# Last 256 tokens of a transformer layer: LayerNorm weights ahead of the transposes, sums on TensorE, mean taken off while the power is made

## The chip, the cores and the metric

The kernel runs on one core of one Trainium2 chip. A core has five engines with queues of their own: TensorE (PE in the profile; its weight loads are PEld), VectorE (DVE), ScalarE (ACT), GpSimd (POOL) and SyncE (SP, which here issues most DMAs). TensorE writes to PSUM, eight banks of 512 fp32 columns by 128 partitions; VectorE and ScalarE read it. The metric is the device time of one execution in microseconds (us). Before the change three runs gave 1610.99 to 1614.45, median 1612.0.

## What is computed

One layer of a diffusion backbone: adaLN modulation, two token mixers (windowed and global attention) on 1024 latent tokens of 1024 features, a LayerNorm, a gated convolutional feed-forward network, and a second LayerNorm. The part that the change touches is the last:

```python
def _layer_norm(x, g, b):
    mu = jnp.mean(xf, axis=-1, keepdims=True)
    var = jnp.mean(jnp.square(xf - mu), axis=-1, keepdims=True)
    return (xf - mu) * lax.rsqrt(var + LN_EPS) * g + b

h = x * (1.0 + scale2) + shift2
y = _conv_ffn(h, w_up, conv_w, conv_b, w_down)
x = _layer_norm(DEEPNORM_ALPHA * x + gate2 * y, ln2_g, ln2_b)
```

## The kernel before

**Layout.** Activations lie with features on the partitions: eight blocks f = 0 to 7 of 128 features, 1024 tokens along the free dimension. `zv(f, s)` is block f of the residual stream for the tokens s. fp32 products are split in a high and a low part of a faster format, so one product is three matmuls (`mm3`, lines 90 to 92).

**Down projection.** It is done as seven block products (`product(p)`, p = 1, 6, 2, 7, 4, 5, and a last one in the open code behind the loop) over NH = 11 contraction steps, each for four blocks of 128 features. `accum` (line 1415, VectorE) adds a finished PSUM tile, times the gate, to z. The last product is cut in tokens: first 512 to 767 (`LN2_S[1]`), then 768 to 1023 (`LN2_S[2]`), the *last tokens*. For tokens 512 to 767 the steps 0 to 6 of all four blocks are issued first (`yl0` to `yl3`), then steps 7 to 10 of each block with its `accum` and `sums`. For the last tokens each block is done in one go, 33 matmuls of 256 columns.

**Second LayerNorm, features on partitions.** For tokens 0 to 511 (b0) and 512 to 767 (b1) `ln_steps` gives a list of steps that `tick` takes up between matmuls by their due times: `stats` (sums over features by one-column products with `onec`, lines 1028 and 1029; then mean, variance and power on VectorE and GpSimd), `diags`, `cast` (line 1044: products with a matrix of ones spread the factors over the partitions, line 1046: ScalarE copies them out of PSUM), and eight `apply` steps (lines 1051 and 1053), after which `emit2` (1408, 1409) applies weight and bias and stores. The same `ln_steps` serve the first LayerNorm (a0, a1, a2), with another pool of PSUM banks.

**Second LayerNorm, last tokens.** Here the tokens are turned onto the partitions. `tok(f)` transposes block f by two matmuls with the identity (line 1538), one per 128 tokens, into `zt[f // 4][t]`; when four blocks are in, VectorE takes `bn_stats` of the bank. `tok(4)` to `tok(7)` are issued with the second half of tokens 512 to 767, `tok(0)` to `tok(3)` one block late with the last tokens' products. After the last one: `bn_aggr`, the power on GpSimd, the shift `nm`, then for four tiles of 128 tokens by 512 features ScalarE normalizes out of PSUM (line 1594) and VectorE or GpSimd multiply by the weight row `lnr[0]` (1583) and add the bias row `lnr[1]` (1585); line 1587 stores.

**What sets the order.** TensorE's instructions are issued in the order of the code (a manual schedule). The other engines' queues are ordered by a scheduler. PSUM banks are named by hand: `sml` takes the next bank of a list `banks`; a tile in a bank waits until the last reader of the tile before it is done. SBUF tiles from `ht` take the slot that has been free longest (`hfree`), and wait for the last access of what lay in it, DMA too.

## Time and profile before

| | us |
|---|---|
| median of 3 runs (lowest, highest) | 1612.0 (1610.99, 1614.45) |
| the profiled execution's own time | 1612.16 |
| its span, first to last instruction | 1610.4 |
| TensorE busy in it | 1536.3 (95%) |
| VectorE, ScalarE, GpSimd busy | 1197.2, 814.6, 745.3 |
| mean granted TensorE clock | 0.988 of full |

How to read the views. The *page* gives busy shares and the chain that ended last. A row of the *timeline* is: start, duration (both us), engine, line, operation, output<-inputs, shapes, count, and in brackets the idle time ahead of it with the instruction that ended it. Rows that belong together are merged (x2, x8). A *windows* row is: stretch and its length, then for PE, PEld, DVE, ACT and POOL the busy time and the number of instructions, the granted clock, the DMA share and GB/s. A *waits* row is: who waited for whom, us in total, times, longest. An fp32 matmul that is not split by hand shows as two records, a fp32 transpose as one. The name `zz` stands for z in the second LayerNorm.

### The profile page before, as it was taken

Reading aid. Unit: us, or ns where it says so; the run is one execution under the profiler, and the core shown is the slowest. Engines: PE = TensorE matmul, PEld = TensorE weight load, DVE = VectorE, ACT = ScalarE, POOL = GpSimd, SP = SyncE. Lnnn points to the kernel's source line nnn. Section 1 sums busy time; section 2 is a strip of 40 time slices with the busy share of each in tenths; the row PEclk is TensorE's granted clock in tenths of the full one; section 3 lists DMA queues with packets and bytes.
Section 4 is the critical chain, followed back from the end, with each engine's and each line's share of the span. In section 5 each row is a group of like instructions: output and inputs, shape, how many; then the busy total and the mean of one; then the engine's idle time right before and its main releaser. Section 6 shows DMA issues by size and latency. Waiting matters only on the chain.

```text
span 1610.4 us, 22060 instructions
## 1 busy us (share of the span) xinstructions
PE 1536.3 (95%) x7680; PEld 1275.4 (79%) x7680; DVE 1197.2 (74%) x1766; ACT 814.6 (51%) x1443; POOL 745.3 (46%) x731
## 2 busy tenths in 40 slices
PE   6999999999999999999999989899999999999996
PEld 5878788888877787777788877688888888888886
DVE  7797646538888777888675787588888888657886
ACT  5422222458887667688322464344544444435542
POOL 0573302526666556655323464366667765021141
PEclk9999999999999999999999999999999999999998
DMA  9695662322237555430560212233334446996821
GB/s 377 214 311 190 214 211 82 121 76 64 62 108 171 126 135 132 114 79 19 174 196 7 87 65 105 92 106 105 105 105 105 106 117 175 370 272 204 260 99 53
DMA packets 112367, 229.98 MB, mean 143 GB/s; under 512 B 12960, under 2 KB 27808, under 8 KB 112160
## 3 DMA queue, kind: packets, MB, share of 16 engines
q1 hardware_dynamic: 96816, 198.93, 37.0%
q0 software_dynamic: 10400, 20.19, 8.1%
q10 hardware_dynamic: 5040, 9.46, 1.6%
q8 instruction: 60, 0.98, 0.3%
q14 instruction: 51, 0.42, 0.1%
HBM read 177.35 MB, written 65.86 MB: 151 GB/s over the span
## 4 chain that ended last, share of the span: by engine, by line
PE 73%; DVE 10%; ACT 4%; issue 4%; DMA 4%; POOL 3%; SPq 0%; ACTq 0%; DVEq 0%; POOLq 0%
PE ptr L531 4%; PE p L92 4%; PE p L91 4%; PE p L90 4%; PE b L92 3%; PE b L91 3%; PE b L90 3%; PE g L90 2%; PE g L91 2%; PE g L92 2%; PE c L90 2%; PE c L92 2%; PE c L91 2%; PE d L90 2%; PE d L92 2%
## 5 line engine op out<-in xcount | busy, mean ns | idle before, releaser
L541 DVE TENSOR_TENSOR ptl<-ptr,pth 128x512 fp32r<-128x512 f32 x188 | 124.8, 686 | 27.7 <-ACT pth L540 25.4
L531 PE MATMUL ptr<-ident,p 128*128 128x128 f32 x816 | 126.8, 278 | 9.4 <-DVE ptl L541 6.9
L540 ACT CAST pth<-ptr 128x512 fp32r<-128x512 f32 x188 | 106.6, 588 | 56.4 <-PE ptr L531 32.8
L87 DVE TENSOR_TENSOR ld<-rd,hd 128x1024 fp32r<-128x1024 f32 x77 | 94.1, 1241 | 52.6 <-ACT hd L82 50.4
L426 ACT ACTIVATE p<-p,nm 128x1024 f32<-128x1024 f32 (+2 forms) x128 | 125.5, 982 | 11.1 <-DVE p L459 10.4
L531 PEld LDWEIGHTS ptr<-ident,p 128*128 128x128 f32 x816 | 93.7, 140 | 39.9 <-DVE ptl L541 14.0
L82 ACT CAST hd<-rd 128x1024 fp32r<-128x1024 f32 x77 | 79.4, 1053 | 81.2 <-PE p L92 51.3
L552 PE MATMUL av<-pth,VT 128*128 128x512 f32 x236 | 104.6, 443 | 1.1 <-ACT avs L558 0.5
L90 PE MATMUL p<-hd 128*128 128x512 f32 x264 | 103.2, 391 | 0.0
L92 PE MATMUL p<-hd,ld 128*128 128x512 f32 x264 | 102.7, 389 | 0.0
L91 PE MATMUL p<-ld,hd 128*128 128x512 f32 x264 | 102.7, 389 | 0.0
L90 PE MATMUL g<-hh,whg 128*128 128x512 f32 x256 | 99.9, 390 | 0.0
L92 PE MATMUL g<-hh,wlg 128*128 128x512 f32 x256 | 99.7, 389 | 0.0
L91 PE MATMUL g<-hl,whg 128*128 128x512 f32 x256 | 99.6, 389 | 0.0
L553 PE MATMUL av<-ptl,VT 128*128 128x512 f32 x236 | 97.7, 414 | 2.0 <-POOL ptl L87 1.9
L87 POOL TENSOR_TENSOR wlg<-wg,whg 128x512 fp32r<-128x512 f32 x32 | 44.4, 1393 | 111.8 <-ACT whg L82 111.8
L459 DVE TENSOR_SCALAR_CACHE_REDUCE p<-s,cvt,nmc 128x1024 f32<-128x1024 f32 x64 | 84.5, 1340 | 12.3 <-PE s L415 11.8
L414 PE MATMUL s<-KL,q 128*128 128x512 f32 (+2 forms) x192 | 76.0, 396 | 2.9 <-ACT p_x L426 2.0
L188 DVE CUSTOM_DVE_ANT_0 wml<-wml,sc,bmc 128x1024 f32<-128x1024 f32 x32 | 44.0, 1387 | 39.3 <-DMA wml<-in_wmodT_dram 38.8
L84 POOL TENSOR_SCALAR pth<-prw 128x512 fp32r<-128x512 f32 x48 | 31.2, 650 | 87.8 <-ACT prw L537 62.2
L82 ACT CAST wA<-ru 128x512 fp32r<-128x512 f32 x57 | 35.6, 625 | 71.4 <-PE d L92 33.7
L415 PE MATMUL s<-KL,q 128*128 128x512 f32 (+2 forms) x192 | 71.7, 373 | 0.0
(396 smaller groups left out, 4997.2 us busy)
## 6 DMA issues: line engine op xcount, KB each, us to landing
wml<-in_wmodT_dram SPq DMA_DIRECT2D x48, 512.0 KB
ru<-in_w_up_dram SPq DMA_DIRECT2D x38, 512.0 KB
rd<-td SPq DMA_DIRECT2D x55, 256.0 KB
rd<-sd SPq DMA_DIRECT2D x44, 256.0 KB
rd<-in_w_dn_dram SPq DMA_DIRECT2D x33, 256.0 KB
wm<-in_wmodT_dram SPq DMA_DIRECT2D x16, 512.0 KB
wg<-in_w_g_dram SPq DMA_DIRECT2D x32, 256.0 KB
sgd<-sg ACTq DMA_DIRECT2D x32, 256.0 KB
```

The source lines that it names most:

```text
L82: nc.scalar.copy(hi, src)
L87: lo_eng.tensor_tensor(out=lo, in0=src, in1=hi.bitcast(F32), op=ALU.subtract)
L90: nc.tensor.matmul(ps, a[0], b[0], start=start, stop=False, skip_group_check=resumed)
L91: nc.tensor.matmul(ps, a[0], b[1], start=False, stop=False, skip_group_check=resumed)
L92: nc.tensor.matmul(ps, a[1], b[0], start=False, stop=stop, skip_group_check=resumed)
L426: nc.scalar.activation(p, s, AF.Exp, bias=nm[:, h:h + 1], scale=scale, accum_out=sm[:, h:h + 1])
L459: nc.vector.tensor_scalar(out=p, in0=o, scalar1=self.qscale(nqs)[:, hs] if self.br else -1.0, scalar2=self.other[:, hs], op0=ALU.mult, op1 ...
L531: nc.tensor.transpose(tr[:, h * P:(h + 1) * P], self.pslice(h, n), ident)
L540: nc.scalar.copy(hi, tr)
L541: nc.vector.tensor_tensor(out=lo, in0=tr, in1=hi.bitcast(F32), op=ALU.subtract)
L552: nc.tensor.matmul(self.av, v, hi, start=first, stop=False)
L553: nc.tensor.matmul(self.av, v, lo, start=False, stop=self.left == 0)
```

## The change

For the last tokens:

- ScalarE makes two copies of each block, z times its weight (`Identity` with a scale) and z squared (`Square`), in `pr` tiles. For block 3 no scaled copy is made: an ordinary product with a diagonal matrix of weights, made beforehand on VectorE, transposes and scales at once.
- `tok(f)` transposes the scaled copy, and four one-column products with `onec` add the block's features and squares of both token tiles into one PSUM tile `st`, which a product with zeros opens. `bn_stats` and `bn_aggr` are gone.
- All eight `tok` are issued with the last tokens' products: 4 and 5 behind the first, 6, 7 and 0 behind the second, 1 behind the third, 2 and 3 behind the fourth.
- The banks are named directly: `zt[1]`, `st` and the small tiles take the four banks of one side, `yl` of both token pieces those of the other, so that the last tokens' products use the banks of `yl2` and `yl3` again, and `zt[0]` those of `yl0` and `yl1`.
- At the end VectorE takes mean times weight off (`lnr[0]`, negated beforehand on GpSimd) while GpSimd makes the power, and then scales and adds the bias in one pass; for one of the four tiles ScalarE scales and GpSimd adds.
- In `cast`, pieces of 256 tokens (a1, a2 and b1) put both broadcast products into the two halves of one bank.

```diff
-OTP = (0, 0), (1, 0)
+OTP = (0, 0),
...
         def cast():
+            both = sml(f"bc{nm}") if 2 * w <= HALF else None
             for i, a in enumerate("rm"):
-                ps = sml(f"bc{a}{nm}")[:, 0:w]
+                ps = sml(f"bc{a}{nm}")[:, 0:w] if both is None else both[:, i * w:(i + 1) * w]
...
-    banks[:] = sides[nside[0] % 2] + sides[nside[0] % 2 ^ 1]
+    yb, ab = sides[nside[0] % 2], sides[nside[0] % 2 ^ 1]
+    banks[:] = [ab[3]]
...
+    hfree += xs
...
+    pr = [ht(f"pr{n}", (P, 4, w)) for n in range(4)]
+    nc.vector.tensor_scalar(out=pr[0][:, 3, 0:P], in0=ident, scalar1=ln2c[:, 3:4], scalar2=None, op0=ALU.mult)
+    nc.gpsimd.tensor_scalar(out=lnr[0], in0=lnr[0], scalar1=-1.0, scalar2=0.0, op0=ALU.mult, op1=ALU.add)
+    zt = {1: [pst(n, f"zt1_{n}") for n in ab[0:2]]}
+    st = pst(ab[2], "stl")
...
+    def prep(f):
+        nc.scalar.activation(pr[2 + f // 4][:, f % 4], zv(f, s), AF.Square)
+        if f != 3:
+            nc.scalar.activation(pr[f // 4][:, f % 4], zv(f, s), AF.Identity, scale=ln2c[:, f:f + 1])
 
     def tok(f):
-        if f % 4 == 0:
-            zt[f // 4] = [sml(f"zt{f}_{t}", keep=True) for t in range(nt)]
+        z, g = zv(f, s), pr[f // 4][:, f % 4]
+        if f == 4:
+            nc.tensor.matmul(st[:, 0:2 * nt], ident, zero4[:, 0:2 * nt], start=True, stop=True)
         for t in range(nt):
-            nc.tensor.transpose(zt[f // 4][t][:, (f % 4) * P:(f % 4 + 1) * P],
-                                zv(f, slice(s.start + t * P, s.start + (t + 1) * P)), ident)
-            if f % 4 == 3:
-                nc.vector.bn_stats(out=bst[:, t, f // 4], in_=zt[f // 4][t])
-
-    todo = [4, 5, 6, 7]
+            ts = slice(t * P, (t + 1) * P)
+            nc.tensor.matmul(st[:, t:t + 1], z[:, ts], onec, start=False, stop=True, skip_group_check=True)
+        for t in range(nt):
+            ts = slice(t * P, (t + 1) * P)
+            o = zt[f // 4][t][:, (f % 4) * P:(f % 4 + 1) * P]
+            if f == 3:
+                nc.tensor.matmul(o, z[:, ts], pr[0][:, 3, 0:P], start=True, stop=True)
+            else:
+                nc.tensor.transpose(o, g[:, ts], ident)
+        for t in range(nt):
+            ts = slice(t * P, (t + 1) * P)
+            nc.tensor.matmul(st[:, nt + t:nt + t + 1], pr[2 + f // 4][:, f % 4, ts], onec, start=False, stop=True,
+                             skip_group_check=True)
...
-    yl = [sml(f"yl{f}")[:, 0:r.stop - r.start] for f in range(4)]
+    yl = [pst(n, f"yl{f}")[:, 0:w] for f, n in enumerate(yb)]
...
         sums(f, r, False)
-        tok(todo.pop(0))
+        prep(f + 4)
+    zt[0] = [pst(n, f"zt0_{n}") for n in yb[0:2]]
...
-    for f in range(4):
-        o = sml(f"yl{f}_{r.start}")[:, 0:r.stop - r.start]
+    for f, done_ in enumerate(((4, 5), (6, 7, 0), (1,), (2, 3))):
+        o = pst(yb[2 + f % 2], f"yl{f}_{r.start}")[:, 0:w]
         last_mm(o, f, r, range(NH))
         accum(f, r, o, True)
-        if todo:
-            tok(todo.pop(0))
-        todo.append(f)
+        prep(f)
+        for n in done_:
+            tok(n)
...
+    nc.vector.tensor_scalar(out=mv, in0=st[:, 0:2 * nt], scalar1=1.0 / D, scalar2=None, op0=ALU.mult)
+    nc.vector.tensor_tensor(out=m2[:, 0:nt], in0=mv[:, 0:nt], in1=mv[:, 0:nt], op=ALU.mult)
+    nc.vector.scalar_tensor_tensor(out=rs[:, 0:nt], in0=mv[:, nt:2 * nt], scalar=LN_EPS, in1=m2[:, 0:nt],
+                                   op0=ALU.add, op1=ALU.subtract)
+    nc.gpsimd.tensor_tensor(out=rs[:, 0:nt], in0=rs[:, 0:nt], in1=mhalf[:, 0:nt], op=ALU.pow)
...
+    for t, a in OTO:
+        o = ot[t, a] = ht(f"ot{t}_{a}", (P, HALF))
+        nc.vector.scalar_tensor_tensor(out=o, in0=lnr[0][:, a], scalar=mv[:, t:t + 1], in1=zt[a][t], op0=ALU.mult,
+                                       op1=ALU.add)
+    for t, a in OTO:
         o = ot[t, a]
-        nc.vector.tensor_tensor(out=o, in0=o, in1=lnr[0][:, a], op=ALU.mult)
-        e = nc.gpsimd if (t, a) in OTP else nc.vector
-        e.tensor_tensor(out=o, in0=o, in1=lnr[1][:, a], op=ALU.add)
+        if (t, a) in OTP:
+            nc.scalar.activation(o, o, AF.Identity, scale=rs[:, t:t + 1])
+            nc.gpsimd.tensor_tensor(out=o, in0=o, in1=lnr[1][:, a], op=ALU.add)
+        else:
+            nc.vector.scalar_tensor_tensor(out=o, in0=o, scalar=rs[:, t:t + 1], in1=lnr[1][:, a], op0=ALU.mult,
+                                           op1=ALU.add)
...
-        o = ot[n] = ht(f"ot{t}_{a}", (P, HALF))
-        nc.scalar.activation(o, zt[a][t], AF.Identity, bias=nm[:, t:t + 1], scale=mv[:, t, 1:2])
```

More of the change, by code (lines that the diff above doesn't have):

```diff
@@ L51 @@
 RAWB = 3
-OTP = (0, 0), (1, 0)
+OTP = (0, 0),
 OTO = (0, 0), (0, 1), (1, 0), (1, 1)
 OTK = 4
-OTA = 1
-OTB = 2
 PSU = 6, 7, 2, 3, 4, 5, 0, 1
@@ L1427, in layer_kernel, with sml @@
     banks = list(PSO)
-    def sml(name, w=512, keep=False):
+    def sml(name, w=512):
         n = banks.pop(0)
-        if not keep:
-            banks.append(n)
+        banks.append(n)
         return ps4.tile([P, w], F32, tag=f"r{n}", name=name)
@@ L1528, in layer_kernel, with pst @@
     nt = w // P
-    zt = {}
-    bst = post.tile([P, nt, 2, 6], F32, tag="bst", name="bst")
-    mv = post.tile([P, nt, 2], F32, tag="bmv", name="bmv")
-    nm = post.tile([P, nt], F32, tag="bnm", name="bnm")
+    def pst(n, name):
+        return ps4.tile([P, HALF], F32, tag=f"r{n}", name=name)
+    pr = [ht(f"pr{n}", (P, 4, w)) for n in range(4)]
[3 more added lines that the diff above has]
+    st = pst(ab[2], "stl")
+    zero4 = post.tile([P, 8], F32, tag="zero4", name="zero4")
+    nc.vector.memset(zero4, 0.0)
+    def prep(f):
+        nc.scalar.activation(pr[2 + f // 4][:, f % 4], zv(f, s), AF.Square)
+        if f != 3:
+            nc.scalar.activation(pr[f // 4][:, f % 4], zv(f, s), AF.Identity, scale=ln2c[:, f:f + 1])
     def tok(f):
-        if f % 4 == 0:
-            zt[f // 4] = [sml(f"zt{f}_{t}", keep=True) for t in range(nt)]
+        z, g = zv(f, s), pr[f // 4][:, f % 4]
+        if f == 4:
+            nc.tensor.matmul(st[:, 0:2 * nt], ident, zero4[:, 0:2 * nt], start=True, stop=True)
         for t in range(nt):
-            nc.tensor.transpose(zt[f // 4][t][:, (f % 4) * P:(f % 4 + 1) * P],
-                                zv(f, slice(s.start + t * P, s.start + (t + 1) * P)), ident)
-            if f % 4 == 3:
-                nc.vector.bn_stats(out=bst[:, t, f // 4], in_=zt[f // 4][t])
-    todo = [4, 5, 6, 7]
+            ts = slice(t * P, (t + 1) * P)
[11 more added lines that the diff above has]
+                             skip_group_check=True)
     def last_mm(o, f, r, ks):
@@ L1571, in layer_kernel @@
     hput(*[f"{a}d3_{k}" for k in range(len(D3AT)) for a in "hl"])
-    hfree += xs
-    tok(3)
-    for t in range(nt):
-        nc.vector.bn_aggr(out=mv[:, t], in_=bst[:, t].rearrange("p a b -> p (a b)"))
-    nc.vector.tensor_scalar(out=mv[:, :, 1], in0=mv[:, :, 1], scalar1=LN_EPS, scalar2=None, op0=ALU.add)
-    nc.gpsimd.tensor_tensor(out=mv[:, :, 1], in0=mv[:, :, 1], in1=mhalf[:, 0:nt], op=ALU.pow)
-    nc.vector.scalar_tensor_tensor(out=nm, in0=mv[:, :, 0], scalar=-1.0, in1=mv[:, :, 1], op0=ALU.mult, op1=ALU.mult)
@@ L1579, in layer_kernel @@
-    ot = {}
-    def last(t, a):
-        o = ot[t, a]
-        nc.vector.tensor_tensor(out=o, in0=o, in1=lnr[0][:, a], op=ALU.mult)
-        e = nc.gpsimd if (t, a) in OTP else nc.vector
-        e.tensor_tensor(out=o, in0=o, in1=lnr[1][:, a], op=ALU.add)
+    sv = [post.tile([P, 2 * nt], F32, tag=f"{n}l", name=f"{n}l") for n in ("mv", "m2", "rs")]
+    mv, m2, rs = sv
+    nc.vector.tensor_scalar(out=mv, in0=st[:, 0:2 * nt], scalar1=1.0 / D, scalar2=None, op0=ALU.mult)
+    nc.vector.tensor_tensor(out=m2[:, 0:nt], in0=mv[:, 0:nt], in1=mv[:, 0:nt], op=ALU.mult)
@@ new lines, in layer_kernel @@
+    nc.vector.scalar_tensor_tensor(out=rs[:, 0:nt], in0=mv[:, nt:2 * nt], scalar=LN_EPS, in1=m2[:, 0:nt],
+                                   op0=ALU.add, op1=ALU.subtract)
+    nc.gpsimd.tensor_tensor(out=rs[:, 0:nt], in0=rs[:, 0:nt], in1=mhalf[:, 0:nt], op=ALU.pow)
+    drain(OTK)
+    ot = {}
+    for t, a in OTO:
+        o = ot[t, a] = ht(f"ot{t}_{a}", (P, HALF))
+        nc.vector.scalar_tensor_tensor(out=o, in0=lnr[0][:, a], scalar=mv[:, t:t + 1], in1=zt[a][t], op0=ALU.mult,
+                                       op1=ALU.add)
@@ L1588, in last @@
                           o.rearrange("p (f q) -> p f q", q=P))
-    drain(OTK)
-    for n in OTO:
-        t, a = n
-        o = ot[n] = ht(f"ot{t}_{a}", (P, HALF))
-        nc.scalar.activation(o, zt[a][t], AF.Identity, bias=nm[:, t:t + 1], scale=mv[:, t, 1:2])
-        drain(max(len(pend) - OTA, 0))
-    for t, a in OTO:
-        last(t, a)
-        drain(max(len(pend) - OTB, 0))
     drain()
```

## The prediction

> **What bounds the kernel now.** I read the page first.

> ```profile
> span 1610.4 us, 22060 instructions
> PE 1536.3 (95%) x7680; PEld 1275.4 (79%) x7680; DVE 1197.2 (74%) x1766; ACT 814.6 (51%) x1443; POOL 745.3 (46%) x731
> PE 73%; DVE 10%; ACT 4%; issue 4%; DMA 4%; POOL 3%; SPq 0%; ACTq 0%; DVEq 0%; POOLq 0%
> ```

> TensorE sets the time, so what it gains or waits counts in full wherever it has no slack. Next come the stretches of the end (columns: PE, PEld, DVE, ACT, POOL busy; then the granted TensorE clock) and TensorE's order there.

> ```profile
> 1567.10:1570.80 3.70, 0.26 (x4) 0.05 (x2) 3.70 (x9) 1.25 (x3) 0.00 (x0) 0.98 0.00 0
> 1570.80:1574.00 3.20, 3.02 (x13) 2.73 (x14) 3.08 (x7) 0.42 (x1) 0.00 (x0) 0.50 0.00 0
> 1582.50:1586.50 4.00, 4.00 (x35) 4.00 (x35) 1.32 (x6) 0.00 (x0) 0.70 (x1) 1.00 0.02 4
> 1606.50:1610.40 3.90, 0.00 (x0) 0.00 (x0) 0.05 (x1) 0.00 (x0) 0.00 (x0) 0.50 0.68 183
> ```
> ```profile
> 1570.80 0.48 PE L1538 MATMUL zt<-ident,zz 128*128 128x128 f32 x1 [3.44 <-DVE zz L1415]
> ...
> 1577.64 0.36 PE L90 MATMUL yl<-hd 128*128 128x256 f32 x1
> ...
> 1581.68 0.28 PE L1028 MATMUL stb<-onec,zs 128*128 128x1 f32 x2
> ...
> 1582.49 0.36 PE L90 MATMUL yl<-hd 128*128 128x256 f32 x1
> 1582.70 0.28 PE L91 MATMUL yl<-ld,hd 128*128 128x256 f32 x1
> ...
> 1586.41 0.28 PE L92 MATMUL yl<-hd,ld 128*128 128x256 f32 x1
> 1586.53 0.38 PE L1538 MATMUL zt<-ident,zz 128*128 128x128 f32 x2
> ...
> 1586.87 0.28 PE L91 MATMUL yl<-ld,hd 128*128 128x256 f32 x1
> ...
> 1595.60 0.28 PE L92 MATMUL yl<-hd,ld 128*128 128x256 f32 x1
> ```

> TensorE stops 3.7 us at the first transposes of the last tokens (their banks are freed late by VectorE), runs 3.2 us at half clock, and is then full until 1595.6. The last 14.8 us, DMA included, have no TensorE work.

> **The change, term by term**, against the profiled span of 1610.4 (1.76 us of the profiled execution's 1612.16 lie outside the span; the median of the runs is 1612.0).

> (a) *The early stop.* The transposes of features 4 to 7 leave the place where TensorE stopped. But the first of the last four outputs now takes the PSUM bank of yl2, so it waits for VectorE's third accumulate.

> ```profile
> 1569.99 2.73 DVE L1415 SCALAR_TENSOR_TENSOR zz<-p,nmod,zz 128x512 f32<-128x512 f32 x4
> ...
> 1572.96 0.49 DVE L1415 SCALAR_TENSOR_TENSOR zz<-yl,nmod,zz 128x256 f32<-128x256 f32 x1
> ...
> 1574.41 0.49 DVE L1415 SCALAR_TENSOR_TENSOR zz<-yl,nmod,zz 128x256 f32<-128x256 f32 x1
> ```

> VectorE gets there without waiting for TensorE: accumulates at 1572.96, 1574.41 and, at the same pitch of 1.45, 1575.86, ending at 1576.35. TensorE would be ready at 1567.1 + 36 products x 0.12 = 1571.4 (0.12: four outputs of 33 products; 33 lie between 1582.49 and 1586.53). So it stands 4.9 us, longer than now, and starts at 1576.35 instead of 1577.64. A stop like that cost 3.2 us at half clock: 15 products at 0.21, then 18 at 0.12, 5.3 us, end at 1581.7. Today that output ends at 1581.68. I take 0. Bounds: no cold clock, -1.4; a cold clock of 7.2 us, as after an earlier stop, +1.7:

> ```profile
> 914.80:922.00 7.20, 7.18 (x35) 7.20 (x36) 2.66 (x8) 1.05 (x1) 0.70 (x1) 0.54 0.19 61
> ```

> (b) *Sums on TensorE.* The kernel already has four such one-column products (stb): from 1581.68 to 1582.70 they and one ordinary product take 1.02, so 0.225 each. Two transposes cost 0.22 (1586.41 to 1586.87 is 0.46, less two products). One feature now takes four sums and two transposes, 1.12. Between 1577.64 and the last product lay two features' transposes, 0.44. Now there lie six features and the zeroing product, 6 x 1.12 + 0.225 = 6.95, all in a stretch where TensorE has no gap. +6.5. Bounds: a sum as cheap as a transpose (0.11), 2.8 less; at half clock, see the rivals.

> (c) *One bank for both broadcasts.* The second broadcast product now waits until ScalarE has copied the first; before, it followed in another bank. This happens three times, once here and twice in the first LayerNorm.

> ```profile
> 1587.82 0.59 PE L1044 MATMUL bcrb<-dgrb,onesf 128*128 128x256 f32 x2
> 1588.25 0.59 PE L1044 MATMUL bcmb<-dgmb,onesf 128*128 128x256 f32 x2
> ```
> ```profile
> 1588.45 0.37 ACT L1046 COPY rbb<-bcrb 128x256 f32<-128x256 f32 x1 [9.74 <-PE bcrb L1044]
> ```
> ```profile
> 924.62 0.59 PE L1044 MATMUL bcma<-dgma,onesf 128*128 128x256 f32 x2
> ```
> ```profile
> 924.87 0.42 ACT L994 ACTIVATE sqa<-z 128x256 f32<-128x256 f32 x1 [1.72 <-PE bcra L1044]
> 925.19 0.36 ACT L1046 COPY rba<-bcra 128x256 f32<-128x256 f32 x1
> ```
> ```profile
> PE b L90 <- ACT T24h L1113: 6.5, 1, 6.5
> PE u L90 <- DVE c L1234: 2.7, 1, 2.7
> PE u L91 <- DVE B L1075: 2.5, 1, 2.5
> ```

> Here the copy ends at 1588.82, so with 0.1 to get across the second starts at 1588.95 for 1588.25: +0.7. Behind it on TensorE stand the products of the third output. At the first place of LayerNorm 1 a square stands ahead of the copy, which ends at 925.55: +1.0, and TensorE has no gap there until the second place. There the extra wait falls ahead of 11.7 us in which TensorE waits anyway for ScalarE and VectorE (last view: TensorE's waits from 940 to 1560). Their chain starts 1.0 later by the first wait and needs the second broadcast only after three products of z; I cost it at 0, at 0.6 without that cover. +1.7; bounds 0.7 and 2.4. [...]

> (d) *The tail.* From the last product to VectorE's last instruction now:

> ```profile
> 1595.92 0.48 DVE L1415 SCALAR_TENSOR_TENSOR zz<-yl,nmod,zz 128x256 f32<-128x256 f32 x1 [1.32 <-PE yl L92]
> 1596.83 1.30 DVE L1541 BATCH_NORM_STATS2 bst<-zt 128x6 f32<-128x512 f32 x2 [0.42 <-PE zt L1538]
> ...
> 1600.53 3.03 DVE L1583 TENSOR_TENSOR ot<-ot,lnr 128x512 f32<-128x512 f32 x3 [0.98 <-ACT ot L1594]
> ...
> 1604.08 1.74 DVE L1583 TENSOR_TENSOR ot<-ot,lnr 128x512 f32<-128x512 f32 x1
> 1605.86 0.69 DVE L1585 TENSOR_TENSOR ot<-ot,lnr 128x512 f32<-128x512 f32 x1
> ```
> ```profile
> 1598.65 0.70 POOL L1577 TENSOR_TENSOR bmv<-bmv,mhalf 128x2 f32<-128x2 f32 x1 [3.45 <-DVE bmv L1576]
> 1601.35 1.66 POOL L1585 TENSOR_TENSOR ot<-ot,lnr 128x512 f32<-128x512 f32 x1 [2.00 <-DVE ot L1583]
> ```

> 1595.60 to 1606.55 is 10.95. New: feature 2's work holds TensorE until 0.12 + 1.12 = 1.24 behind the last product (feature 3's accumulate, ready at 0.80, is hidden behind it). Feature 3 takes four sums and two ordinary products of 128 columns, 0.9 + 0.43 (one broadcast of 256 columns takes 0.43, so 0.215 each): 2.57, and 0.2 until VectorE has it. Then on VectorE: three tiny steps of 0.2, four mean subtractions of 0.7 to 0.75 (the power, 0.7 on POOL, lies under three of them), three last passes of 0.69 and some 1.0 lost to POOL's one remaining add (1604.08: 1.74 for 0.69): 6.5. Sum 9.25, so -1.7. Bounds: all seven large passes at the 1.0 of the group at 1600.53, +0.4; no loss to POOL, -2.7. The DMA behind it, 3.85, stays.

> (e) *At nothing.*

> ```profile
> 1578.29 0.42 ACT L994 ACTIVATE sqb<-zz 128x256 f32<-128x256 f32 x1 [1.23 <-DVE zz L1415]
> ```
> ```profile
> 1561.80 4.63 DVE L87 TENSOR_TENSOR ld<-rd,hd 128x1024 fp32r<-128x1024 f32 x4 [3.57 <-ACT hd L82]
> ```
> ```profile
> 1412.04 0.91 POOL L1211 DMA_DIRECT2D td<-rd  x1 [29.23 <-DMA rd<-g2d]
> ```

> Fifteen more ScalarE passes over 256 columns (0.42 each as this square, 6.3 us) go mostly where ScalarE idles (9.74 us ahead of the copy at 1588.45); the last square runs beside feature 2's sums, else 0.4. The diagonal weight tile stands on VectorE ahead of the 3.57 us wait for the last casts, else under the 0.49 of an accumulate twice as wide. The negated weight row stands on POOL ahead of the stores to td, in the 29 us that POOL idles; uncovered some 3 us (1.66 for 512 columns, twice). Their buffers held the first half's output, whose stores have to land first (3.85 us at the end of the span); the last products of yl and the casts lie in between. No DMA is added; the queue's order differs only in which output piece goes first.

> Sum: 0 + 6.5 + 1.7 - 1.7 = +6.5: span 1616.9, runs 1612.0 + 6.5 = **1618.5**. With the bounds taken together, 1615.0 to 1622.5.

> **Rivals.**
> 1. *The end of LayerNorm 1 gets shorter* (not slower). The three waits above, 11.7 us, are for VectorE and ScalarE, whose order there the change also shuffles, with POOL's: a third piece of z is scaled before the mean comes off, POOL takes z3 ahead of B4. If 3.3 us of the waits go, the kernel is within 0.2%; if 9.7 go, it is faster by more than that: half of them (5.9) gives 1612.6. Against it: the same number of passes, a mean that comes later.
> 2. *The sums cool the clock.* The stretches of sums and transposes are 3.4 us long, twice. If the clock falls to half behind each for 3.2 us, 15 products lose 0.09 each, 1.4 twice: 1621.3. For it: the stop of 3.7 us did it. Against it: eight sums, at 0.225 1.8 us, and the products behind them kept the full clock:

> ```profile
> 1535.70:1541.00 5.30, 5.30 (x33) 4.62 (x33) 3.34 (x8) 1.54 (x2) 1.03 (x1) 1.00 0.59 195
> ```

> [...]
> 3. *The tail does not shorten*, so the change does not do what it says: VectorE's passes at 1.0 each, 1620.2.
> 4. *The sums hide behind weight loads*: 2.8 less in (b), 1615.7. The stb rows speak against it.

> **How the numbers follow.** Forecast 0.58, rival 1 0.14 (0.04 of it faster), rival 2 0.14, rival 3 0.08, rival 4 0.06. A difference under 0.2% (3.2 us) can't be told from none. Slower: forecast, rivals 2 and 3, and most of rival 4, 0.84; same 0.12; faster 0.04. The 8 in 10 run from 1615.0, the lower bounds, to 1622.0, past rival 2.

> **What would show it.** (a): TensorE without the stop at 1567, but one of 4 to 5 us ahead of the first 768 output, released by VectorE's accumulate, half clock behind it. (b): 0.2 to 0.24 between sums, one feature 1.1. (c): ScalarE's copy named as releaser of the second broadcast, three times. (d): 9 to 9.5 us from the last product to VectorE's end. I am wrong if the last product ends less than 4 us later than now, or if the waits behind LayerNorm 1 shrink by more than 3.

## The result, and the profile after

Eight runs of each kernel, side by side: 1612.4 us before (1609.9 to 1614.5), 1619.4 after (1614.8 to 1625.1), ratio 1.0043, 95% interval 1.0025 to 1.0061. The kernel became slower by 7.0 us, where 6.5 were forecast. A second set of eight runs of the same kernel gave 1616.8 against 1611.1 before, ratio 1.0031 (1.0019 to 1.0044), so the two sets put the loss between 5 and 7 us.

The page of the kernel after, the lines that were shown of before:

```profile
span 1618.4 us, 22204 instructions
PE 1545.6 (95%) x7748; PEld 1283.5 (79%) x7748; DVE 1199.0 (74%) x1764; ACT 816.8 (50%) x1455; POOL 746.4 (46%) x731
...
PE 78%; DVE 9%; ACT 4%; issue 4%; POOL 3%; DMA 2%; SPq 0%; DVEq 0%; ACTq 0%; POOLq 0%
```

TensorE is busy 9.3 us longer and its share of the chain that ended last rises from 73 to 78%: what was added stands on the engine that sets the time. Its order at the end (timeline of TensorE; columns as in the prediction):

```profile
1575.44 0.58 PE L88 MATMUL yl<-hd 128*128 128x256 f32 x1 [4.55 <-DVE zz L1414]
...
1581.87 0.28 PE L1026 MATMUL stb<-onec,zs 128*128 128x1 f32 x2
...
1585.72 0.56 PE L88 MATMUL yl<-hd 128*128 128x256 f32 x1
...
1592.12 0.50 PE L1553 MATMUL stl<-onec,zz 128*128 128x1 f32 x4
...
1593.10 0.58 PE L1553 MATMUL stl<-onec,zz 128*128 128x1 f32 x4
...
1596.38 0.59 PE L1043 MATMUL bcb<-dgrb,onesf 128*128 128x256 f32 x2
1597.44 0.70 PE L1043 MATMUL bcb<-dgmb,onesf 128*128 128x256 f32 x2 [0.46 <-ACT rbb L1045]
```

The stop at 1567 is gone and a longer one, 4.55 us from 1570.89 on, is released by VectorE's accumulate. One feature of sums and transposes takes 1592.12 to 1593.10, 0.98. But the 33 products from 1585.72 to 1592.12 take 6.40 us where 33 took 4.04 before: most of them run at half clock. The windows view shows it, cut at steps of 3.41 us (PE, PEld, DVE, ACT, POOL busy, then the granted clock):

```profile
1570.62:1574.03 3.41, 0.27 (x3) 0.07 (x1) 3.28 (x7) 0.42 (x1) 0.00 (x0) 1.00 0.00 0
1574.03:1577.45 3.42, 2.01 (x9) 2.01 (x10) 3.07 (x8) 1.25 (x3) 0.00 (x0) 0.50 0.00 0
1577.45:1580.86 3.41, 3.41 (x18) 3.41 (x17) 0.27 (x1) 0.00 (x0) 0.00 (x0) 0.50 0.00 0
1580.86:1584.27 3.41, 3.41 (x33) 3.41 (x31) 1.01 (x5) 0.81 (x2) 0.70 (x1) 1.00 0.00 0
1584.27:1587.69 3.42, 3.42 (x18) 3.42 (x18) 0.79 (x3) 0.00 (x0) 0.00 (x0) 0.50 0.02 5
1587.69:1591.10 3.41, 3.41 (x18) 3.41 (x18) 0.00 (x0) 0.00 (x0) 0.00 (x0) 0.50 0.00 0
1591.10:1594.51 3.41, 3.41 (x34) 3.41 (x34) 0.48 (x1) 0.81 (x2) 0.00 (x0) 1.00 0.00 0
```

Between these edges the granted clock is constant. Two windows at half clock come with the stop (it fills 3.14 us of the window before them and 1.41 of the first of the two), and two follow the first group of sums: rival 2 of the prediction, which had 0.14. Last, VectorE's tail:

```profile
1608.36 0.16 DVE L1596 TENSOR_SCALAR mvl<-stl 128x4 f32<-128x4 f32 x1 [1.81 <-PE stl L1563]
...
1609.47 2.06 DVE L1605 SCALAR_TENSOR_TENSOR ot<-lnr,mvl,zt 128x512 f32<-128x512 f32 x3
1611.45 2.85 DVE L1613 SCALAR_TENSOR_TENSOR ot<-ot,rsl,lnr 128x512 f32<-128x512 f32 x3
```

It ends at 1614.30, 8.56 behind the last product at 1605.74.

So that the runs below can be compared, I cut each profiled span at four instructions that every kernel has: the first product of tokens 512 to 767 (`yl`), the first sum of their LayerNorm (`stb`), the last product of the last tokens, and VectorE's last instruction. What lies between the starts of the first three and the end of the last (us), beside the time of the runs; each ratio is to the kernel before on the same chip, whose median lay between 1611.1 and 1612.4:

| kernel | median (runs) | ratio to before, 95% | yl to stb | stb to last product | last product to VectorE's end | behind it |
|---|---|---|---|---|---|---|
| before | 1612.4 (8) | | 26.00 | 13.92 | 10.95 | 3.82 |
| after | 1619.4 (8) | 1.0043, 1.0025 to 1.0061 | 26.97 | 23.87 | 8.56 | 4.13 |
| after again (e9) | 1616.8 (8) | 1.0031, 1.0019 to 1.0044 | 26.73 | 20.83 | 8.55 | 4.12 |
| e1 other banks | 1616.2 (12) | 1.0032, 1.0019 to 1.0046 | 23.35 | 23.70 | 8.55 | 4.13 |
| e2 sums left out | 1611.8 (12) | 1.0000, 0.9987 to 1.0014 | 26.08 | 15.69 | 8.56 | 4.13 |
| e3 sums three times | 1627.8 (4) | 1.0113, 1.0087 to 1.0138 | 26.77 | 30.73 | 8.56 | 4.12 |
| e4 before, new cast | 1614.1 (12) | 1.0015, 1.0004 to 1.0026 | 26.14 | 14.65 | 10.94 | 3.81 |
| e5 sums spread | 1618.5 (6) | 1.0040, 1.0027 to 1.0052 | 27.06 | 20.82 | 8.56 | 4.12 |
| e6 tail undone | 1623.0 (6) | 1.0066, 1.0049 to 1.0084 | 26.50 | 20.82 | 10.78 | 3.81 |
| e7 few sums | 1607.7 (12) | 0.9968, 0.9958 to 0.9978 | 24.14 | 14.31 | 8.72 | 4.13 |
| e8 few sums, zeroed | 1608.1 (12) | 0.9982, 0.9966 to 0.9997 | 24.92 | 13.92 | 8.72 | 4.14 |
| e10 spread again | 1616.5 (10) | 1.0033, 1.0022 to 1.0044 | 26.97 | 20.83 | 8.56 | 4.14 |

What lies ahead of `yl` is left out of it: that product starts at 1554.90 in the first profile of the kernel after and at 1558.90 in the second, so a term of 1 us can't be read there. Five to ten windows at half clock lie ahead of `yl` in these twelve profiles (six in the first of the kernel after, seven in the second), and the two profiles with ten, e8 and e10, reach `yl` last, at 1562.85 and 1562.01. Runs of one kernel differ by several us, part of it there, and the columns tell more than the medians.

### The profile page after: what moved, and what is told of

The parts are those of the page before. It is cut to its first block, busy times and chain, and to the rows that moved or that the text cites. A ratio compares the mean times of both kernels' runs of the same rounds, so it can differ in the third digit from the quotient of the medians.

```text
span 1618.4 us, 22204 instructions
## 1 busy us (share of the span) xinstructions
PE 1545.6 (95%) x7748; PEld 1283.5 (79%) x7748; DVE 1199.0 (74%) x1764; ACT 816.8 (50%) x1455; POOL 746.4 (46%) x731
## 4 chain that ended last, share of the span: by engine, by line
PE 78%; DVE 9%; ACT 4%; issue 4%; POOL 3%; DMA 2%; SPq 0%; DVEq 0%; ACTq 0%; POOLq 0%
PE ptr L529 5%; PE p L88 4%; PE p L89 4%; PE p L90 3%; PE g L88 3%; PE g L89 3%; PE g L90 3%; PE b L90 3%; PE b L89 3%; PE b L88 3%; PE c L88 2%; PE c L89 2%; PE c L90 2%; PE d L89 2%; PE d L90 2%
## 5 line engine op out<-in xcount | busy, mean ns | idle before, releaser
L424 ACT ACTIVATE p<-p,nm 128x1024 f32<-128x1024 f32 (+2 forms) x128 | 125.4, 982 | 10.9 <-DVE p L457 10.1
L90 PE MATMUL p<-hd,ld 128*128 128x512 f32 x264 | 102.7, 389 | 0.0
L90 PE MATMUL g<-hh,wlg 128*128 128x512 f32 x256 | 99.8, 390 | 0.0
L82 POOL TENSOR_SCALAR pth<-prw 128x512 fp32r<-128x512 f32 x48 | 31.1, 647 | 88.3 <-ACT prw L535 62.7
```

The costliest lines, as they stand in the source:

```text
L90: nc.tensor.matmul(ps, a[1], b[0], start=False, stop=stop, skip_group_check=resumed)
L424: nc.scalar.activation(p, s, AF.Exp, bias=nm[:, h:h + 1], scale=scale, accum_out=sm[:, h:h + 1])
```

## The experiments

**e1: the bank of the first output.** Against the kernel after:

```diff
-    zt[0] = [pst(n, f"zt0_{n}") for n in yb[0:2]]
+    zt[0] = [pst(n, f"zt0_{n}") for n in yb[2:4]]
-        o = pst(yb[2 + f % 2], f"yl{f}_{r.start}")[:, 0:w]
+        o = pst(yb[f % 2], f"yl{f}_{r.start}")[:, 0:w]
```

> The last tokens' outputs take the banks of yl0 and yl1 instead of yl2 and yl3, and zt[0] those of yl2 and yl3; nothing else is changed against the kernel after. In its profile TensorE came to the first last-token output at 1570.7 and waited until 1575.44 for the third accumulate; the first accumulate ended at 1572.66. Own theory (step a: the wait for yl2's bank is a cost of its own, and a stop of over 3 us is what cools the clock behind it): the stop shrinks from 4.6 to about 2.0 us, no half clock directly behind it, 2.7 + 2.2 = 4.9 us less than the kernel after; the second stretch at half clock (1584 to 1591, 3.1 us of loss) stays, because the sums make it. Rival A (the stop does not cool the clock by its length, any stop does): 2.7 us less. Rival B (the second stretch at half clock is a late effect of the stop, not of the sums): both stretches go, 8.0 us less.

TensorE's timeline in this kernel, the row behind the stop:

```profile
1577.62 0.39 PE L88 MATMUL yl<-hd 128*128 128x256 f32 x1 [1.82 <-DVE zz L1414]
```

The stop went from 4.55 to 1.82, 2.73 less, as both theories had it, so the third accumulate was the cause. But half clock still followed, for one window instead of two, so my "no half clock behind a short stop" was wrong; yl to stb became 3.4 to 3.6 shorter, between the two numbers. Its windows show what cooled:

```profile
1575.59:1579.01 3.42, 1.60 (x13) 1.39 (x13) 3.27 (x8) 0.42 (x1) 0.00 (x0) 1.00 0.00 0
1579.01:1582.42 3.41, 3.41 (x18) 3.41 (x17) 3.09 (x8) 1.25 (x3) 0.00 (x0) 0.50 0.00 0
1582.42:1585.83 3.41, 3.41 (x33) 3.41 (x32) 1.49 (x7) 0.82 (x2) 0.70 (x1) 1.00 0.00 0
1585.83:1589.25 3.42, 3.42 (x18) 3.42 (x17) 0.52 (x2) 0.00 (x0) 0.00 (x0) 0.50 0.02 5
...
1592.66:1596.07 3.41, 3.41 (x34) 3.41 (x33) 0.00 (x0) 0.78 (x2) 0.00 (x0) 1.00 0.00 0
1596.07:1599.49 3.42, 2.96 (x11) 2.06 (x10) 1.18 (x4) 0.74 (x2) 0.04 (x1) 0.50 0.00 0
```

A window in which TensorE stood 1.82 of 3.42 is followed by one at half clock. The two windows that end at 1585.83 and 1596.07 are wholly busy, with 2.67 and 2.36 us of sums and transposes in them (1583.16 to 1585.83, and 1592.66 to 1595.02), and the clock falls behind both. Rival B is gone with that: these half clocks belong to the sums, not to the stop. In the medians the gain can't be seen against the scatter.

**e2: the sums left out.** The loops over the one-column products run only for features 2 and 3:

```diff
-        for t in range(nt):
+        for t in range(nt if f in (2, 3) else 0):
```

> The sums of features and squares on TensorE are left out for features 0, 1 and 4 to 7 of the last tokens (24 one-column products; those of features 2 and 3 stay, and all transposes). Own theory (step b, with the clock: a sum costs 0.225, and sums also cool the clock once): 24 x 0.225 = 5.4 less, and the second stretch at half clock goes too, 3.1 more, together 8.5 us less than the kernel after. Rival (the second stretch at half clock comes from the stop before it): 5.4 us less, and products at half clock remain between 1583 and 1591. Rival (sums hide behind weight loads, as transposes do): 2.6 us less.

The kernel leaves the sums of six blocks out of mean and variance. The clock stayed full from stb to the last product, which took 15.69. Against the second profile of the kernel after, which also kept full clock there, 5.14 less: the price of 24 sums, 0.21 each; against the first, 8.18 less, the difference being the half clock. The stop of 4.55 was there, and no half clock between 1583 and 1591. That alone doesn't put the rival of the stop out, since the second profile of the kernel after, sums and all, kept full clock there too; e1 and e3 do. The rival of 2.6 us (hidden sums) is out. By the ratios the kernel is 5 to 7 us faster than the kernel after and equals the kernel before.

**e3: more sums.** In the same loops:

```diff
+        for t in list(range(nt)) * (3 if f in (6, 7, 0) else 1):
```

> The sums of features 6, 7 and 0 are issued three times (24 more one-column products, in the second group of sums, which ran at full clock in the kernel after; the mean and variance come out wrong by that). Price alone: 24 x 0.225 = 5.4 us more than the kernel after. If a long stretch of sums by itself cools the clock: the stretch becomes 8.5 us long, the clock falls to half inside it or behind it, and the sum is 5.4 + 3 or more, 8.5 to 11 us more. If the clock falls only where a stop came shortly before: 5.4, with the products of the third output at 0.12 apart.

Windows of this kernel, in the group of sums that lasts from 1590.88 to 1602.33:

```profile
1592.69:1596.10 3.41, 3.41 (x33) 3.41 (x33) 0.00 (x0) 0.00 (x0) 0.00 (x0) 1.00 0.00 0
1596.10:1599.51 3.41, 3.41 (x18) 3.41 (x19) 0.00 (x0) 0.00 (x0) 0.00 (x0) 0.50 0.00 0
...
1602.93:1606.34 3.41, 2.95 (x11) 2.23 (x11) 0.45 (x2) 0.37 (x1) 0.00 (x0) 0.50 0.00 0
```

A window filled with sums and a few transposes (3.16 and 0.25 us), far from any stop, is followed by half clock, and it lasts for three windows, the last of them right behind the window in which the sums end (1602.33). Stb to the last product is 30.73, 9.9 above the second profile of after: 5.1 for the sums by e2's price, 4.8 for the clock. So in this run a long stretch of sums (3.16 us in a window of 3.41) cools the clock by itself.

**e4: the cast alone**, put into the kernel before:

```diff
         def cast():
+            both = sml(f"bc{nm}") if 2 * w <= HALF else None
             for i, a in enumerate("rm"):
-                ps = sml(f"bc{a}{nm}")[:, 0:w]
+                ps = sml(f"bc{a}{nm}")[:, 0:w] if both is None else both[:, i * w:(i + 1) * w]
```

> The kernel before with one part of the change alone: pieces of 256 tokens put both broadcast products into one bank. Own theory (step c): the second broadcast waits for ScalarE's copy at three places, 0.9 and 0.7 in the first LayerNorm, of which about 0.6 comes back in the waits behind it, and 0.6 in the second: 1.0 to 1.7 us more than the kernel before. Rival (the wait is hidden behind waits that are there anyway): 0 to 0.6. Rival 1 of the prediction (the shuffle of the first LayerNorm shortens its waits): faster by 3 or more.

By the runs 0.6 to 4.2 us more (the interval), 1.9 by the medians; stb to the last product +0.73. TensorE's waits behind the first LayerNorm in this kernel (who waited for whom, us, times, longest):

```profile
PE u L91 <- DVE B L1076: 1.4, 1, 1.4
PE u L91 <- POOL B L1076: 1.3, 1, 1.3
PE bca L1045 <- ACT rba L1047: 1.3, 2, 0.8
```

The second broadcast waits for ScalarE's copy, as forecast. Before, the first two waits were 2.5 and 0.9; of 3.4 us 0.7 come back. Rival 1 falls, since nothing gets faster. The interval of the runs begins just where the other rival's range ends (0.6); what speaks against it is the 0.73 behind stb, which nothing on TensorE's path gives back.

**e5 and e10: the same sums, spread.** Against the kernel after, the work of a feature stands between contraction steps:

```diff
+    mid = {(1, 4): 4, (2, 3): 6, (2, 7): 7, (3, 3): 0, (3, 7): 1}
-    for f, done_ in enumerate(((4, 5), (6, 7, 0), (1,), (2, 3))):
+    for f, done_ in enumerate(((), (5,), (), (2, 3))):
-        last_mm(o, f, r, range(NH))
+        for k in range(NH):
+            last_mm(o, f, r, (k,))
+            if (f, k) in mid:
+                tok(mid[f, k])
```

> The kernel after with the same sums and transposes in other places: the features' work stands singly between contraction steps of the last tokens' second to fourth outputs (4, 6, 7, 0 and 1 inside an output, 5 behind one, 2 and 3 at the end as before), so that no more than 1.1 us of it follow one another before the last product. Own theory (a dense stretch of sums cools the clock): the price of the sums stays, the stretches at half clock that follow the sums go (two quanta of 3.4 us in the profile of after, 3.1 us of loss), 1.5 to 3 us less than the kernel after over many runs, the profile with no half clock between 1583 and the last product. Rival (sums cool the clock however they are placed, or half clock comes from the stop): as the kernel after, within 1 us.

> The kernel with its sums spread, on the same chip as the kernel after. Own theory: no window holds more than 1.5 us of sums, so none cools; the mean granted clock of the runs is higher by about 0.001, the median 1 to 2 us below that of the kernel after beside it. Rival (sums cool the clock wherever they stand): no difference in the clock and the time.

Both profiles kept full clock from stb to the last product (20.82 and 20.83). But in time it gained nothing: on the same chip 1.0033 against 1.0031 of the kernel after, 1616.5 against 1616.8. My expectation of 1 to 2 us was not borne out: the half clock behind sums is real, but no loss of that size shows in the median. What share of the kernel after's runs has it is left open.

**e6: the tail undone.** The power first, then as before the change:

```diff
-        nc.vector.scalar_tensor_tensor(out=o, in0=lnr[0][:, a], scalar=mv[:, t:t + 1], in1=zt[a][t], op0=ALU.mult,
-                                       op1=ALU.add)
+        nc.scalar.activation(o, zt[a][t], AF.Identity, scale=rs[:, t:t + 1])
...
+        nc.vector.scalar_tensor_tensor(out=o, in0=lnr[0][:, a], scalar=m2[:, t:t + 1], in1=o, op0=ALU.mult, op1=ALU.add)
+        e = nc.gpsimd if (t, a) in ((0, 0), (1, 0)) else nc.vector
+        e.tensor_tensor(out=o, in0=o, in1=lnr[1][:, a], op=ALU.add)
```

> The kernel after with its tail undone: the power comes first, ScalarE then scales the four tiles out of PSUM, VectorE takes mean times power times weight off, and the bias is added by GpSimd for two tiles and VectorE for two, as before the change. Own theory (step d): 10.9 to 11.3 us from the last product to VectorE's last instruction instead of the 8.6 of the kernel after, so 1.7 to 2.4 us more than the kernel after. Rival 3 (the change's tail does not shorten): no difference.

VectorE's timeline of this kernel:

```profile
1608.14 0.16 DVE L1601 TENSOR_TENSOR m2l<-mvl,rsl 128x2 f32<-128x2 f32 x1 [0.81 <-POOL rsl L1600]
1608.86 3.08 DVE L1609 SCALAR_TENSOR_TENSOR ot<-lnr,m2l,ot 128x512 f32<-128x512 f32 x3 [0.56 <-ACT ot L1606]
```

VectorE waits 0.81 for the power and 0.56 for ScalarE, and the passes beside GpSimd's adds take 3.08 for three. From the last product 10.78, 2.22 more than the kernel after, of which 0.3 comes back behind it. So the new tail is worth 1.9 us; rival 3 is out. The runs of e6 lie further up than that, 4.4 us by the medians above e5, which ran on the same chip, but the two intervals overlap, and what more there may be stays open.

**e9: the kernel after again.**

> The kernel after unchanged, as a partner on the same chip for the kernel with few sums and the one with its sums spread, and for a second profile. Own theory (the clock is set anew every 3.41 us, by what TensorE did in the 3.41 us before, on a grid whose place differs from run to run; a window with more than about 2.4 us of sums and transposes, or 1.9 us of idleness, is followed by one at half clock): all stretches at half clock last whole multiples of 3.41 us, their number behind the two groups of sums differs from the first profile or not by where the grid lies, and the spans of the runs scatter with the mean granted clock by some 1.6 us for each 0.001. Rival (the half clock behind the first group of sums in the first profile belongs to this kernel's order and comes every time): two such windows from about 1584 in every profile, and runs as tight as those of the kernel before.

Its windows across the sums (stb starts at 1585.63, the second group is 1592.83 to 1595.94):

```profile
1584.31:1587.72 3.41, 3.41 (x32) 3.41 (x32) 0.97 (x4) 0.81 (x2) 0.46 (x1) 1.00 0.00 0
1587.72:1591.13 3.41, 3.41 (x31) 3.41 (x31) 0.83 (x3) 0.00 (x0) 0.24 (x1) 1.00 0.02 5
1591.13:1594.55 3.42, 3.42 (x34) 3.42 (x32) 0.48 (x1) 0.82 (x2) 0.00 (x0) 1.00 0.00 0
```

The same program, and no half clock behind the sums: the first group is cut by an edge at 1587.72, and no window of the two groups holds more than 2.1 us of sums and transposes. So the rival ("this order does it every time") is out. The spans of these eight runs (1612.5 to 1619.1 at a mean clock of 0.987 to 0.990) don't follow the clock as they did in the first set (1613.0 at 0.990 to 1623.3 at 0.984), so that the scatter is all clock is not shown.

**e7 and e8: fewer sums.** From here on GpSimd and VectorE add features and squares, and TensorE takes eight one-column products.

```diff
+    def pre(f, e):
+        q = pr[2 + f // 4][:, f % 4]
+        e.tensor_tensor(out=zs2[:, s], in0=zv(4, s) if f == 5 else zs2[:, s], in1=zv(f, s), op=ALU.add)
+        e.tensor_tensor(out=zq2[:, s], in0=pr[3][:, 0] if f == 5 else zq2[:, s], in1=q, op=ALU.add)
...
+    for n in (5, 6, 7):
+        pre(n, nc.gpsimd)
+    for n in (4, 5, 6, 7):
+        tok(n)
...
+    for f, done_ in enumerate(((), (0,), (1,), (2, 3))):
+        o = pst(yb[f % 2], f"yl{f}_{r.start}")[:, 0:w]
         last_mm(o, f, r, range(NH))
         accum(f, r, o, True)
         prep(f)
+        if f != 3:
+            pre(f, nc.vector)
```

with two banks for the broadcasts again, and `tok` without sums.

> The kernel after with three parts replaced, the tail kept: features and squares of the last tokens are added up on GpSimd (4 to 7) and VectorE (0 to 2), so that TensorE makes 8 one-column products instead of 32 and no zeroing product; outputs take the banks of yl0 and yl1, and the transposes of 4 to 7 stand in the stop ahead of the first output; each broadcast has a bank of its own, as in the kernel before. Own theory, against the kernel after: 24 x 0.225 + 0.22 = 5.6 for the sums, 1.5 to 3 for the clock behind them, 2.7 for the stop, 1.0 to 1.7 for the broadcasts, 10.8 to 13.0 less; against the kernel before 4 to 6 us less (1606 to 1608 where that is 1612). If the clock still falls to half behind the shorter stop, that loss of about 1.5 to 2.4 is in both and nothing changes by it. Rival (the adds on GpSimd and VectorE delay the accumulates or the second LayerNorm's passes, which share these engines): the last product ends no earlier than 1595.6 + 0, as before, and only the tail's 2 us are won.

> The kernel with few sums, with the zeroing product of the kernel after put back ahead of the eight one-column products, which then all add. 0.2 us more than without it: 4 to 5 us less than the kernel before (ratio about 0.997), 11 to 12 less than the kernel after, which runs beside it. If the tail, now reached earlier, were held by the stores of tokens 512 to 767 ahead of it in SP's queue, less than 3 us would be left.

In e7 each of the first four one-column products carried the start flag and there was no zeroing product, and its mean and variance are not those of all features, for a reason that no row of a profile shows; e8 computes the whole. TensorE's timeline of e8:

```profile
1579.81 0.30 PE L1551 MATMUL zt<-ident,pr 128*128 128x128 f32 x1 [0.97 <-DVE zz L1413]
1580.38 0.98 PE L1551 MATMUL zt<-ident,pr 128*128 128x128 f32 x7 [0.27 <-DVE zz L1413]
1582.42 0.58 PE L88 MATMUL yl<-hd 128*128 128x256 f32 x1 [1.06 <-DVE zz L1413]
...
1602.03 0.28 PE L1603 MATMUL stl<-zero,ident 128*128 128x4 f32 x2
...
1604.30 0.69 PE L1549 MATMUL zt<-pr,zz 128*128 128x128 f32 x4
```

The transposes stand in the stop, and TensorE idles there 2.30 us in three pieces (4.55 in the kernel after); the nine products of the sums take 2.27 at the end (1602.03 to 1604.30). Stb to the last product is 13.92 again, as before the change, with the short tail kept. Against the kernel before, e8 is 0.03 to 0.34% faster (some 3 us by the ratio), e7 0.2 to 0.4%; I had expected 4 to 5 for e8; its four cuts add up to -3.0. It beats both kernels, the one before narrowly; against the kernel after on the same chip the medians are 8.7 apart, where 11 to 12 were expected. The profile of e8 is its slowest run (span 1614.5): it reaches `yl` at 1562.85, where the kernel before did at 1555.68 with the same work for TensorE up to there. One window at half clock follows its stop (1581.97 to 1585.38).

The rival is partly right. VectorE's adds for tokens 512 to 767, first in the kernel after, then in e8, where GpSimd adds at the same time:

```profile
1567.21 0.42 DVE L994 TENSOR_TENSOR zq<-zq,sqb 128x256 f32<-128x256 f32 x1
```
```profile
1575.10 0.87 POOL L1559 TENSOR_TENSOR zq<-pr 128x256 f32<-128x256 f32 x1
```
```profile
1575.29 0.95 DVE L994 TENSOR_TENSOR zq<-zq,sqb 128x256 f32<-128x256 f32 x1
...
1581.89 0.47 DVE L1413 SCALAR_TENSOR_TENSOR zz<-yl,nmod,zz 128x256 f32<-128x256 f32 x1
```

Four such adds in e8 lie beside GpSimd's, and three of them take some 0.95 instead of 0.42. The first accumulate of tokens 512 to 767 then comes 19.04 us behind `yl`; in the kernel after it came at 17.28 (1572.18), and within 0.01 of that in every profile but those of e7 and e8. All three pieces of the stop in e8 are released by accumulates, so the adds on GpSimd cost up to 1.8 us there (an estimate from these rows; no run moves them elsewhere), about what is missing from the 4 to 5. Still the last product comes 38.84 behind `yl`, where it came 39.92 behind it before, so more than the tail was won.

## Why the prediction was right, and where it was not

The sum of the forecast from `yl` on is 0 + 6.5 + 0.7 - 1.7 = 5.5. The second profile of the kernel after has 0.73 + 6.91 - 2.40 + 0.30 = 5.54; the first has 0.97 + 9.95 - 2.39 + 0.31 = 8.84, 3.04 of it half clock behind sums. The mechanism was the forecast one in all four terms: each has its wait or its price in the rows, and a run that changes it alone (e1, e2, e4, e6). But that the sum came out at 5.54 is partly luck: (a) was 0.73 too low, (b), (c) and (d) with what lies behind it were 0.2, 0.1 and 0.4 too high, and the misses cancel. Whole spans tell less: the first grew by 8.1, since that execution reached `yl` 0.8 us earlier than the kernel before, the second by 8.8, since it reached it 3.2 us later. The half clock behind the sums, which the forecast left to a rival, is in one of the two profiles; its share in the 7.0 is not known.

**(a) The early stop, 0: right in kind, 0.1 to 1.1 too low.** VectorE's rows after:

```profile
1572.18 0.48 DVE L1414 SCALAR_TENSOR_TENSOR zz<-yl,nmod,zz 128x256 f32<-128x256 f32 x1
...
1574.91 0.48 DVE L1414 SCALAR_TENSOR_TENSOR zz<-yl,nmod,zz 128x256 f32<-128x256 f32 x1
```

The third accumulate ends at 1575.39 and the product starts at 1575.44: the wait for yl2's bank, 4.55 for the 4.9 forecast. (The stop of the kernel before that I read as 3.7 us is 3.44 in its own row.) The step that was short is the cold clock: I took 3.2 us from the stop before, and two windows came, 6.8 us, of which 5.4 fell on products. That is inside the bound that I took from the stop in LayerNorm 1. It depends on where the edges lie: of the seven profiles with this order up to stb, e2 has the same stop of 4.55 and one window at half clock behind it, and there yl to stb is 26.08, as forecast; the six others have two windows and 26.50 to 27.06. e1 shows that the bank was the cause.

**(b) Sums, +6.5: right without the clock.** 20.83 less 13.92 less 0.63 for the broadcast is 6.28. A sum was priced at 0.225, and e2 gives 0.21. Rival 4 is out.

**Rival 2, the clock behind the sums: it is real, and comes in some executions.** The price that I gave it (1.4 for each 3.2 us, 2.8 for two) is what the first profile shows (3.04), both windows behind the first group; its place and its frequency were wrong ("behind each"). The row of eight sums that I held against it, at full clock, was no evidence: the half clock of that profile begins at 1570.68, by steps of 3.41 us an edge lies at 1536.55, and it cuts those sums (1535.74 to 1537.44) in two parts of 0.8 and 0.9 us, less than in any wholly busy window that cooled.

**(c) The broadcasts, +1.7: confirmed, by another path.** TensorE's rows in the first LayerNorm after:

```profile
921.59 0.59 PE L1043 MATMUL bca<-dgra,onesf 128*128 128x256 f32 x2
923.00 0.70 PE L1043 MATMUL bca<-dgma,onesf 128*128 128x256 f32 x2 [0.82 <-ACT rba L1045]
...
937.45 0.59 PE L1043 MATMUL bca<-dgra,onesf 128*128 128x256 f32 x2
938.50 0.70 PE L1043 MATMUL bca<-dgma,onesf 128*128 128x256 f32 x2 [0.46 <-ACT rba L1045]
```

Start to start 1.41, 1.05, and 1.06 in the second LayerNorm, for 0.43: +0.98, +0.62, +0.63, against 1.0, 0 (0.6 without cover) and 0.7. The second is paid in full on the spot, and its cover shows further on, in TensorE's waits:

```profile
PE u L88 <- DVE c L1233: 3.0, 1, 3.0
...
PE u L89 <- DVE B L1074: 1.4, 1, 1.4
PE u L89 <- POOL B L1074: 1.3, 1, 1.3
```

2.7, 2.5 and 0.9 before: the wait for B shrinks by 0.7, the wait for c varies (2.7 in the second profile, 1.5 in e2, 4.2 in e4). So a net of some 0.9 in the first LayerNorm, for the 1.0 forecast. Rival 1 wanted 3.3 us off these waits; there is no sign of it.

**(d) The tail, -1.7: larger, -2.4, less 0.3 behind it.** The term that was mis-sized is the seven large passes and their company: 6.5 was forecast from the sums' arrival to VectorE's end, and 5.94 was measured (1608.36 to 1614.30). The mean subtractions come 0.66 apart (forecast 0.70 to 0.75), and the loss to GpSimd's add is smaller: the three last passes take 2.85, where 3.1 were forecast. VectorE has the sums 2.62 behind the last product (2.77 forecast). The 0.3 behind it I had not seen. SyncE issues the last four stores within 2.31 us instead of 3.92, and in e6, where it is 3.92 again, the stretch behind VectorE's end is back at 3.81; that the closer stores cause it is argued from this alone. (Rival 3 at 1620.2 takes the tail as unchanged; passes at 1.0 each would by my own bound of +0.4 have been 1620.6.)

**(e) At nothing**: no wait of TensorE for the ScalarE passes, the diagonal tile or the weight row shows at the end, and e2, which keeps them all, equals the kernel before in time, to within its interval of 2 us either way.

## What to carry to other kernels

Reductions put on TensorE by one-column products cost 0.21 us each here; on the engine that sets the time, add up first on an engine that idles and reduce once, and look what the adds there slow down (in e8 three of VectorE's adds beside GpSimd's took some 0.95 us instead of 0.42). Before a bank or buffer is reused, look who frees it and when: here another bank, with nothing else changed, was free 2.7 us earlier. A part that shortens the tail is worth having even if the rest of its change is not: e8 keeps it and drops the rest.

## What was not expected of the hardware

```profile
872.14:875.55 3.41, 3.24 (x23) 2.70 (x22) 1.37 (x4) 0.00 (x0) 0.34 (x2) 1.00 0.00 0
875.55:878.96 3.41, 3.41 (x10) 2.65 (x9) 1.36 (x3) 0.00 (x0) 1.02 (x1) 0.50 0.00 0
```
```profile
1571.87:1575.28 3.41, 1.57 (x14) 1.36 (x12) 3.38 (x7) 0.52 (x2) 0.00 (x0) 1.00 0.00 0
1575.28:1578.69 3.41, 0.71 (x6) 0.71 (x7) 3.09 (x8) 1.25 (x3) 0.00 (x0) 1.00 0.00 0
```

The window at 872.14 holds 1.97 us of one-column sums (each counted up to the start of the next instruction, a zeroing product as one of them) and 0.17 of idleness, and half clock follows, as it does behind the same window in e1 and e10. Of the windows that were busy throughout, those with 1.85 us of sums (e1, 1592.66), 2.16 (the first profile of after, 1580.86), 2.29 and 3.16 were followed by half clock, and those with 1.89 (the same profile, 1591.10) and 1.92 (e3, 1582.44) were not. So for sums the boundary in these profiles lies near 1.9 us in 3.41. With the transposes counted in there is none to be seen: my "2.4 us of sums and transposes" in the expectation of e9 doesn't hold, since the windows with 1.97 cooled and one with 2.39 didn't. For idleness it lies close by: 1.71 us (e9, 788.99) and 1.82 (e1) sufficed, and the 1.84 in the window at 1571.87 did not. Both are a little over half of a window, and neither is sharp. The windows named here ahead of a half clock were idle for only part of their length, the ones with sums for 0.17 us at most.
